# A decoder layer's attention stage: one store for the sums of four heads, and three kinds of stores issued from GpSimd instead of SyncE

## The chip, the cores and the metric

The kernel runs on one core of a Trainium2 chip. The core has a matrix engine (TensorE, in the profile PE; its weight loads are PEld), VectorE (DVE), ScalarE (ACT), GpSimd (POOL) and SyncE (SP), each with an instruction stream of its own, executed in order. They meet only through semaphores. Data moves between DRAM and the on-chip memory, and from one set of partitions to another, by DMA. A DMA is issued as an instruction of one engine's stream and carried out by 16 DMA engines. The metric is device time in microseconds; three runs of the kernel before gave 1806.03, 1810.8 and 1818.87 us, so the median is 1810.8 us.

## The reference

A decoder layer on x of 1024 tokens by 1024 channels, in float32. What matters here is branch A, differential attention with 8 heads of two softmax maps each:

```python
s = jnp.einsum('bqhcd,bkhcd->bhcqk', qblk, kf) * scale
s = s + bias[None, :, None]                    # ALiBi, and -max where the key is later than the query
p = jax.nn.softmax(s, axis=-1)
a = p[:, :, 0] - lam * p[:, :, 1]
out = jnp.einsum('bhqk,bkhe->bqhe', a, vf)
...
a = rms_norm(a, subln_g[l]) * (1.0 - lam_init)      # per head, over its 128 channels
y_attn = a.reshape(B, S, DIFF_V_WIDTH) @ w_attn_branch[l]
...
gates = jax.nn.sigmoid(gate_logits)
mix = gates[:, :, 0] * y_attn + gates[:, :, 1] * y_pool + gates[:, :, 2] * y_mem
x = x + rms_norm(mix @ w_out[l], norm_mix_post[l])
```

Around it stand a pooling branch, a cross attention into 256 memory tokens, and a channel mixer with a convolution. They are untouched.

## The kernel before

Every float32 product is made as three products of a high and a low part (`split` and `mm3`, lines 83 to 96), so a projection of a 128-channel block is 3 x 8 matmuls per 512 tokens (`proj_half`). Results that are too large to stay on chip go through DRAM tensors: `ao_d` (attention outputs, one row block per head), `gate_d` (logits of the first gate), `ss_d` (sums of squares of the attention outputs), `sum_d` (sums of the first map's exponentials) and `r_d` (the scales worked out of the last two).

The attention stage (lines 706 to 958) goes over 8 heads and, in a head, over 4 blocks `b` of 256 queries, each of two halves `u` of 128 queries. `t = 2b + u` numbers the 128-query tiles. For each half:

- `scores` (line 788) multiplies queries with keys for the two maps `c`, adds the bias and takes the negative maximum on VectorE (line 812), and takes the exponential in place on ScalarE (line 817), whose accumulator gives the row sums: `sm[:, 0:1]` for the first map, `sm[:, 1:2]` for the second. Line 819 stores the first column, 128 numbers, to `sum_d` from SP.
- `combine` (line 824) forms z0 - lam * (sum0 / sum1) * z1 on VectorE; the division by sum0 is left for later.

For each block, `turn_weights` (line 836) transposes the weights on TensorE, `weigh_values` (line 852) multiplies them with the values, copies the result `po` to `ao` and stores it to `ao_d` (line 867, 128 KB, 32 times), and squares it. `head_norm` (line 878) sums the squares over the channels with a matmul of ones and stores one row to `ss_d` (line 885, 1 KB, 32 times). After four heads, `load_norms` (line 890) reads both small tensors back and `head_norms` (line 897) works out the scales.

Beside this work the loop weaves fillers for the next head: `queries_keys(h + 1)` (line 737) loads the weights `raw` (line 322, 512 KB for the queries and again for the keys), projects on TensorE, splits on ScalarE and VectorE into `qtmp` and `ktmp`, and moves these by DMA to the partitions where the scores want them (`q<-qtmp`, line 752, 8 transfers a head; `ks<-ktmp`, line 767, 8 transfers a head). `values(h + 1)` loads the head's values (line 732). `gate(dt)` (line 773) projects a 128-channel block of the first gate's logits and stores it in two halves to `gate_d` (line 781, 256 KB, 16 times in all): five blocks during the heads, three after them. The tiles `qtmp`, `ktmp` and `g0` come from one tag with two buffers (`gq`, tag `"t"`), so a tile is free for its next writer when the transfer out of it has landed.

Order: `weave` lists the stages and fillers, and a planner then settles the order of the instructions on each engine before the run; at run time each engine and each queue executes its list in order, and an instruction whose inputs are not ready holds up all that stand behind it. All DMAs of the kernel are issued from SP, so the stores of the attention stage and the loads for the next head stand in one list. An on-chip tile is given to its next user when the semaphore of its last reader, a DMA's landing included, has been seen.

Of the kernel before, what the change touches and what calls it, by code (L numbers as in the profile page):

```python
# [8 lines left out]
F32 = mybir.dt.float32  # L9
F32R = mybir.dt.float32r  # L10
I32 = mybir.dt.int32
AF = mybir.ActivationFunctionType
ALU = mybir.AluOpType
AX = mybir.AxisListType

P = 128
D = 1024
S = 1024
KT = D // P
H4 = KT // 2  # L20
H = 512
NM = 256
NH = 8
# [15 lines left out]
def kernel(  # L39
# [7 lines left out]
    nc = tc.nc  # L47
# [12 lines left out]
    out = out[0]  # L60
# [6 lines left out]
    small = ctx.enter_context(tc.tile_pool(name="small", bufs=6, side="left"))  # L67
# [6 lines left out]
    def bank(shape=(P, H), name="b1"):  # L74
        return ps1.tile(list(shape), F32, tag="b1", name=name)
# [186 lines left out]
    ident = const.tile([P, P], F32, name="ident")  # L262
# [18 lines left out]
    nlam = const.tile([P, 1], F32, name="nlam")  # L281
# [17 lines left out]
    gate_d = dram.tile([KT, P, S], F32, name="gate_d")  # L299
    ao_d = dram.tile([NH, P, S], F32, name="ao_d")  # L300
# [6 lines left out]
    ss_d = dram.tile([NH, S], F32, name="ss_d")  # L307
# [465 lines left out]
    def gate(dt):  # L773

        wh, wl = wsplit(chunk(w_in, C_G + dt * P), [P, KT, P])
        for i in range(2):
            pg = pbank(name="pg0")
            proj_half(pg, wh, wl, i)
            g = gq.tile([P, H], F32, tag="t", name="g0")
            nc.scalar.activation(out=g, in_=pg, func=AF.Copy)  # L780
            nc.sync.dma_start(out=gate_d[dt][:, i * H:(i + 1) * H], in_=g)
            yield

    zts, ats, pns, exps, last, ends = {}, {}, {}, {}, {}, {}

    biases = {}

    def scores(h, b, u):

        qs, ks = qktiles[h]  # L790
        t = 2 * b + u
        n = (t + 1) * P
        parts = 1 if n <= H else 2
        m = n // parts
        q = qs[t // 4]
        ts = slice((t % 4) * P, (t % 4 + 1) * P)
        mx = small.tile([P, 2], F32, tag="mx", name="mx")
        sm = small.tile([P, 2], F32, tag="sm", name="sm")
        z2 = []

        def halves(a):
            return a.rearrange("p (a m) -> p a m", a=parts)

        for c in range(2):
            pss = bank2(name="pss2")
            for i in range(parts):
                keys = ks[c][:, i * m:(i + 1) * m]
                for j in range(2):
                    nc.tensor.matmul(pss[:, i * H:i * H + m], q[:, j, c, ts], keys, start=(j == 0), stop=(j == 1))  # L809
            z = ap_.tile([P, S], F32, tag="z%d" % c, name="z", bufs=3 - c)  # L810
            o = 896 - t * P
            nc.vector.tensor_tensor_reduce(  # L812
                out=halves(z[:, 0:n]), in0=pss.rearrange("p (a m) -> p a m", a=2)[:, 0:parts, 0:m],
                in1=halves(biases[h][:, o:o + n]), scale=1.0, scalar=3.0e38,
                op0=ALU.add, op1=ALU.min, accum_out=mx[:, c:c + 1])
            z2.append(z)
            nc.scalar.activation(out=z[:, 0:n], in_=z[:, 0:n], func=AF.Exp, scale=-1.0,  # L817
                                 bias=mx[:, c:c + 1], accum_out=sm[:, c:c + 1])
        nc.sync.dma_start(out=sum_d[h, t * P:(t + 1) * P].rearrange("(p o) -> p o", o=1), in_=sm[:, 0:1])
        exps[h, b, u] = z2, mx, sm  # L820
        if b == 3 and u == 1:
            qktiles.pop(h)

    def combine(h, b, u):

        z2, mx, sm = exps.pop((h, b, u))
        n = (2 * b + u + 1) * P
        nc.vector.reciprocal(out=mx[:, 1:2], in_=sm[:, 1:2])
        nc.vector.scalar_tensor_tensor(
            out=mx[:, 0:1], in0=mx[:, 1:2], scalar=sm[:, 0:1], in1=nlam, op0=ALU.mult, op1=ALU.mult)  # L830
        last["combine"] = nc.vector.scalar_tensor_tensor(
            out=z2[0][:, 0:n], in0=z2[1][:, 0:n], scalar=mx[:, 0:1], in1=z2[0][:, 0:n],
            op0=ALU.mult, op1=ALU.add)
        zts[h, b, u] = z2[0]

    def turn_weights(h, b):

        zs = [zts.pop((h, b, u)) for u in range(2)]
        ats[h, b] = []
        for k2 in range(b + 1):  # L840
            at = [ap_.tile([P, 4 * P], F32R, tag="aT", name="aT%d" % j, bufs=9) for j in range(2)]
            pt = bank((P, 4 * P), "pta")

            todo = [(kk, u) for kk in range(2) for u in range(2) if (k2, kk, u) != (b, 1, 0)]
            for j, (kk, u) in enumerate(todo):
                k = 2 * k2 + kk
                nc.tensor.transpose(pt[:, j * P:(j + 1) * P], zs[u][:, k * P:(k + 1) * P], ident)
            n = len(todo) * P
            split(at[0][:, 0:n], at[1][:, 0:n], pt[:, 0:n])
            ats[h, b].append(at)  # L850

    def weigh_values(h, b):
        at = ats.pop((h, b))
        vh, vl = vtiles[h]
        bs = slice(b * 2 * P, (b + 1) * 2 * P)
        po = bank((P, 2 * P), "poa")

        parts = [(k, slice(0, 2 * P), at[k // 2], slice((k % 2) * 2 * P, (k % 2 + 1) * 2 * P))
                 for k in range(2 * b + 1)]
        terms = [(part, i, j) for part in parts for i, j in ((0, 0), (0, 1), (1, 0))]  # L860
        last = (2 * b + 1, slice(P, 2 * P), at[b], slice(2 * P, 3 * P))
        terms[1:1] = [(last, i, j) for i, j in ((0, 0), (0, 1), (1, 0))]
        for n, ((k, qs, w, ws), i, j) in enumerate(terms):
            nc.tensor.matmul(po[:, qs], (vh, vl)[i][:, k, :], w[j][:, ws], start=(n == 0), stop=(n == len(terms) - 1))  # L864
        ao = ap_.tile([P, 2 * P], F32, tag="ao", name="ao", bufs=2)
        nc.scalar.activation(out=ao, in_=po, func=AF.Copy)
        nc.sync.dma_start(out=ao_d[h][:, bs], in_=ao)

        sq = ap_.tile([P, 2 * P], F32, tag="sq", name="sq", bufs=1)
        nc.scalar.activation(out=sq, in_=po, func=AF.Square)  # L870
        sqs = [ap_.tile([P, 2 * P], F32R, tag="sq%d" % j, name="sq%d" % j, bufs=1) for j in range(2)]
        nc.scalar.activation(out=sqs[0], in_=sq, func=AF.Copy)
        ends["square"] = nc.vector.tensor_tensor(out=sqs[1], in0=sq, in1=sqs[0].bitcast(F32), op=ALU.subtract)
        pns[h, b] = sqs
        if b == 3:
            vtiles.pop(h)

    def head_norm(h, b):
        sqs = pns.pop((h, b))
        pn = bank((P, 2 * P), "pn")  # L880
        for j in range(2):
            nc.tensor.matmul(pn, ones, sqs[j], start=(j == 0), stop=(j == 1))
        srow = ap_.tile([1, 2 * P], F32, tag="srow", name="srow", bufs=2)
        nc.scalar.activation(out=srow, in_=pn[0:1, :], func=AF.Copy)  # L884
        nc.sync.dma_start(out=ss_d[h:h + 1, b * 2 * P:(b + 1) * 2 * P], in_=srow)

    HG = NH // 2
    hns = {}

    def load_norms(g):  # L890

# [27 lines left out]
    for h in range(NH):  # L919
        if h + 1 < NH:  # L920
            head_bias(h + 1)
        stages = []
        for b in range(4):
            n = 4 * h + b
            stages.append(lambda h=h, b=b: scores(h, b, 0))
            if n >= 1:
                def weights(n=n):
                    combine(*blocks[n - 1], 1)
                    turn_weights(*blocks[n - 1])
                stages.append(weights)  # L930
            stages.append(lambda h=h, b=b: scores(h, b, 1))
            stages.append(lambda h=h, b=b: combine(h, b, 0))
            if n >= 2:
                stages.append(lambda n=n: head_norm(*blocks[n - 2]))
            if n >= 1:
                stages.append(lambda n=n: weigh_values(*blocks[n - 1]))
            if h == HG and b == 1:
                stages.append(lambda: load_norms(0))
            if h == HG and b == 3:
                def norms():  # L940
                    with tc.issue_after(last["combine"].ins):
                        head_norms(0)
                stages.append(norms)
        fillers = []
        if h + 1 < NH:
            fillers += steps(queries_keys(h + 1), 4)
            for n, step in enumerate(steps(values(h + 1), 2)):
                fillers.insert(2 * n + 1, step)
        for dt in GATES[h]:
            fillers += steps(gate(dt), 2)  # L950
        weave(stages, fillers)
    combine(*blocks[-1], 1)
    turn_weights(*blocks[-1])
    head_norm(*blocks[-2])
    weigh_values(*blocks[-1])
    head_norm(*blocks[-1])
# [424 lines left out]
```

## Time and profile before

One execution was profiled. Its own time, 1826.35 us, differs a little from the three timed runs.

| | us |
|---|---|
| median of three runs | 1810.8 |
| profiled execution | 1826.35 |
| its span, first to last instruction | 1824.6 |
| TensorE busy | 1745.2 |
| VectorE busy | 1238.9 |
| ScalarE busy | 863.3 |
| GpSimd busy | 4.4 |
| attention stage, 510 to 973 us of the span | 463 |
| TensorE busy in it | 412.77 |

All times in a profile count from the first instruction. Issuing a DMA and waiting for a semaphore are not counted as busy. The chain of waits starts from the last instruction and goes back, at each step to what released it; a piece called DMA runs from the issue of a transfer to its landing. "SPq" is the instruction queue of SP. A list of waits names the engine and line that waited, what ended the wait, the microseconds in total, how often, and the longest.

### The profile page before, as it was taken

To read this page: it belongs to the slowest core of one execution; us is meant where nothing else is said; L and a number is where in the kernel's file an instruction comes from. 1 tells how busy PE (TensorE), PEld (TensorE's weight loads), DVE (VectorE), ACT (ScalarE), POOL (GpSimd) and SP (SyncE) were. 2 spreads that over 40 slices of the span, in tenths; PEclk is the share of its full clock that TensorE was granted. 3 is DMA by queue.
4 is the path that set the end of the run, shared out by engine and by line. 5 is a ranking of instruction groups with operands and counts; after the bars stand their busy time and mean duration, and the time that the engine had idled before them with its cause. 6 is when DMAs were issued, how large, how long until landed. Compare 5 with 4: busy or idle time off the path is not lost.

```text
span 1824.6 us, 22737 instructions
## 1 busy us (share of the span) xinstructions
PE 1745.2 (96%) x8208; PEld 1451.3 (80%) x8208; DVE 1238.9 (68%) x2159; ACT 863.3 (47%) x1502; POOL 4.4 (0%) x27
## 2 busy tenths in 40 slices
PE   6999999999988899889899999999999999999997
PEld 5888888888866778768787788888888888888886
DVE  8775866666544656646665556676888888878476
ACT  6344454444434545535563333364555555543452
POOL 0000000000000000000000000000000000000000
PEclk9999999999998999989999999999999999999999
DMA  7783454353594666866737566175333433483343
GB/s 244 262 317 131 153 171 152 116 174 115 144 163 111 119 106 114 126 99 118 116 65 233 185 204 173 47 229 175 116 97 117 122 104 96 140 313 116 105 146 130
DMA packets 239430, 271.89 MB, mean 149 GB/s; under 512 B 23681, under 2 KB 173398, under 8 KB 237910
## 3 DMA queue, kind: packets, MB, share of 16 engines
q1 hardware_dynamic: 239318, 270.44, 53.4%
q8 instruction: 65, 1.06, 0.3%
q14 instruction: 47, 0.39, 0.1%
HBM read 176.45 MB, written 68.78 MB: 134 GB/s over the span
## 4 chain that ended last, share of the span: by engine, by line
PE 74%; DMA 14%; DVE 6%; ACT 3%; issue 2%; SPq 1%; DVEq 0%; ACTq 0%
PE pa L94 6%; PE pa L96 6%; PE pa L95 6%; PE pb L94 4%; PE pb L96 4%; PE pb L95 4%; DMA ks<-ktmp 3%; DMA sum_d<-sm 2%; DMA raw<-in_w_in_dram 2%; PE poa L864 2%; PE pss L809 2%; PE pqk L95 2%; PE pqk L94 2%; PE pqk L96 2%; PE pe L96 2%
## 5 line engine op out<-in xcount | busy, mean ns | idle before, releaser
L812 DVE CUSTOM_DVE_ANT_0 z<-pss,hbias 128x256 f32<-128x256 f32 (+7 forms) x128 | 94.2, 753 | 58.3 <-PE pss L809 57.3
L86 ACT ACTIVATE wh<-raw 128x1024 fp32r<-128x1024 f32 (+1 forms) x64 | 60.9, 951 | 132.0 <-PE pqk L95 34.6
L1159 DVE SCALAR_TENSOR_TENSOR cvt<-gv,cols,cvt 128x1023 f32<-128x1023 f32 x88 | 112.5, 1279 | 15.6 <-ACT cvt L1155 14.3
L86 ACT ACTIVATE wpage<-s 128x512 fp32r<-128x512 f32 x120 | 75.2, 627 | 89.9 <-PE pb L96 33.6
L94 PE MATMUL pqk<-hTh,wh 128*128 128x512 f32 x256 | 104.1, 407 | 11.7 <-ACT wh L86 11.7
L809 PE MATMUL pss<-ks,q 128*128 128x512 f32 (+5 forms) x384 | 91.7, 363 | 24.1 <-DMA ks<-ktmp 18.0
L817 ACT ACTIVATE z<-z,mx 128x256 f32<-128x256 f32 (+7 forms) x128 | 98.8, 773 | 32.5 <-DVE mx L812 31.5
L87 DVE TENSOR_TENSOR wl<-raw,wh 128x1024 fp32r<-128x1024 f32 (+1 forms) x64 | 69.6, 1087 | 63.2 <-ACT wh L86 50.2
L87 DVE TENSOR_TENSOR wpage<-s,wpage 128x512 fp32r<-128x512 f32 x120 | 82.1, 690 | 41.2 <-ACT wpage L86 41.1
L94 PE MATMUL pa<-T,wpage 128*128 128x512 f32 x264 | 102.8, 389 | 0.9 <-DVE gv L244 0.9
L95 PE MATMUL pqk<-hTl,wh 128*128 128x512 f32 x256 | 103.2, 403 | 0.0
L96 PE MATMUL pqk<-hTh,wl 128*128 128x512 f32 x256 | 103.1, 403 | 0.0
L96 PE MATMUL pa<-T,wpage 128*128 128x512 f32 x264 | 102.7, 389 | 0.0
L95 PE MATMUL pa<-T,wpage 128*128 128x512 f32 x264 | 102.7, 389 | 0.0
L809 PEld LDWEIGHTS pss<-ks,q 128*128 128x128 f32 x384 | 68.1, 202 | 37.0 <-DVE mx L812 11.5
L86 ACT ACTIVATE page<-blk 128x1024 fp32r<-128x1024 f32 (+1 forms) x42 | 41.4, 988 | 85.5 <-PE pe L95 50.6
L87 DVE TENSOR_TENSOR page<-blk,page 128x1024 fp32r<-128x1024 f32 (+1 forms) x42 | 47.6, 1134 | 39.2 <-ACT page L86 39.2
L94 PE MATMUL pd<-page 128*128 128x512 f32 x176 | 69.3, 394 | 2.0 <-ACT row L1269 2.0
L95 PE MATMUL pd<-page 128*128 128x512 f32 x176 | 69.1, 393 | 0.0
L96 PE MATMUL pd<-page 128*128 128x512 f32 x176 | 68.9, 392 | 0.0
L94 PEld LDWEIGHTS pqk<-hTh,wh 128*128 128x128 f32 x256 | 49.7, 194 | 20.0 <-ACT wh L86 12.0
L864 PE MATMUL poa<-aT,v 128*128 128x256 f32 (+1 forms) x480 | 62.2, 281 | 0.5 <-ACT srow L884 0.5
(383 smaller groups left out, 4877.2 us busy)
## 6 DMA issues: line engine op xcount, KB each, us to landing
raw<-in_w_in_dram SPq DMA_DIRECT2D x32, 512.0 KB
q<-qtmp SPq DMA_DIRECT2D x64, 256.0 KB
wd<-in_w_down_dram SPq DMA_DIRECT2D x22, 512.0 KB
tw_d<-wd SPq DMA_DIRECT2D x11, 1024.0 KB
rawv<-in_w_up_dram SPq DMA_DIRECT2D x22, 512.0 KB
rawu<-in_w_up_dram SPq DMA_DIRECT2D x22, 512.0 KB
ff_d<-cvt SPq DMA_DIRECT2D x22, 512.0 KB
blk<-ff_d SPq DMA_DIRECT2D x20, 512.0 KB
```

The costliest lines, as they stand in the source:

```text
L86: nc.scalar.activation(out=hi, in_=src, func=AF.Copy)
L87: nc.vector.tensor_tensor(out=lo, in0=src, in1=hi.bitcast(F32), op=ALU.subtract)
L94: nc.tensor.matmul(o, ah, bh, start=first, stop=False, skip_group_check=onto)
L95: nc.tensor.matmul(o, ah, bl, start=False, stop=False, skip_group_check=onto)
L96: nc.tensor.matmul(o, al, bh, start=False, stop=last, skip_group_check=onto)
L809: nc.tensor.matmul(pss[:, i * H:i * H + m], q[:, j, c, ts], keys, start=(j == 0), stop=(j == 1))
L812: nc.vector.tensor_tensor_reduce(out=halves(z[:, 0:n]), in0=pss.rearrange("p (a m) -> p a m", a=2)[:, 0:parts, 0:m], in1=halves(biases[h][ ...
L817: nc.scalar.activation(out=z[:, 0:n], in_=z[:, 0:n], func=AF.Exp, scale=-1.0, bias=mx[:, c:c + 1], accum_out=sm[:, c:c + 1])
L864: nc.tensor.matmul(po[:, qs], (vh, vl)[i][:, k, :], w[j][:, ws], start=(n == 0), stop=(n == len(terms) - 1))
L1159: nc.vector.scalar_tensor_tensor(out=cv[:, sh:], in0=u[:, 0:S - sh], scalar=w, in1=cv[:, sh:], op0=ALU.mult, op1=ALU.add)
```

## The change

A tile `sums` of 128 partitions by 8 heads by 8 query tiles is allocated once for the whole stage. The exponential of the first map accumulates into its column `[:, h, t]` instead of into `sm`, which keeps only the second map's sum; `combine` reads the column there. The store of 128 numbers per half (64 in all) goes away. In its place `turn_sums(g)` transposes the 32 columns of four heads on TensorE, copies the result to a row tile on ScalarE and stores it to `sum_d` in one DMA from SP, for the first four heads at the start of the fifth, and for the other four after the last block's `turn_weights`. The stores to `gate_d`, `ao_d` and `ss_d` are issued from GpSimd's queue instead of SP's. The values computed are the same.

```diff
-            nc.sync.dma_start(out=gate_d[dt][:, i * H:(i + 1) * H], in_=g)
+            nc.gpsimd.dma_start(out=gate_d[dt][:, i * H:(i + 1) * H], in_=g)
...
+    sums = ap_.tile([P, NH, KT], F32, name="sums", bufs=1)
...
-        sm = small.tile([P, 2], F32, tag="sm", name="sm")
+        sm = small.tile([P, 1], F32, tag="sm", name="sm")
...
-                                 bias=mx[:, c:c + 1], accum_out=sm[:, c:c + 1])
-        nc.sync.dma_start(out=sum_d[h, t * P:(t + 1) * P].rearrange("(p o) -> p o", o=1), in_=sm[:, 0:1])
+                                 bias=mx[:, c:c + 1], accum_out=sm if c else sums[:, h, t:t + 1])
...
-        nc.vector.reciprocal(out=mx[:, 1:2], in_=sm[:, 1:2])
+        t = 2 * b + u
+        n = (t + 1) * P
+        nc.vector.reciprocal(out=mx[:, 1:2], in_=sm)
         nc.vector.scalar_tensor_tensor(
-            out=mx[:, 0:1], in0=mx[:, 1:2], scalar=sm[:, 0:1], in1=nlam, op0=ALU.mult, op1=ALU.mult)
+            out=mx[:, 0:1], in0=mx[:, 1:2], scalar=sums[:, h, t:t + 1], in1=nlam, op0=ALU.mult, op1=ALU.mult)
...
-        nc.sync.dma_start(out=ao_d[h][:, bs], in_=ao)
+        nc.gpsimd.dma_start(out=ao_d[h][:, bs], in_=ao)
...
-        nc.sync.dma_start(out=ss_d[h:h + 1, b * 2 * P:(b + 1) * 2 * P], in_=srow)
+        nc.gpsimd.dma_start(out=ss_d[h:h + 1, b * 2 * P:(b + 1) * 2 * P], in_=srow)
...
+    def turn_sums(g):
+
+        pt = bank((P, P), "ptn")
+        nc.tensor.transpose(pt[0:HG * KT, :], sums[:, g * HG:(g + 1) * HG].rearrange("p h t -> p (h t)"), ident)
+        row = ap_.tile([HG * KT, P], F32, tag="trow", name="trow", bufs=1)
+        nc.scalar.activation(out=row, in_=pt[0:HG * KT, :], func=AF.Copy)
+        nc.sync.dma_start(out=sum_d[g * HG:(g + 1) * HG].rearrange("h (t p) -> (h t) p", p=P), in_=row)
...
+            if h == HG and b == 0:
+                stages.append(lambda: turn_sums(0))
             if h == HG and b == 1:
                 stages.append(lambda: load_norms(0))
...
     turn_weights(*blocks[-1])
+    turn_sums(1)
     head_norm(*blocks[-2])
```

More of the change, by code (lines that the diff above doesn't have):

```diff
@@ L826, in combine @@
         z2, mx, sm = exps.pop((h, b, u))
-        n = (2 * b + u + 1) * P
-        nc.vector.reciprocal(out=mx[:, 1:2], in_=sm[:, 1:2])
+        t = 2 * b + u
+        n = (t + 1) * P
+        nc.vector.reciprocal(out=mx[:, 1:2], in_=sm)
         nc.vector.scalar_tensor_tensor(
-            out=mx[:, 0:1], in0=mx[:, 1:2], scalar=sm[:, 0:1], in1=nlam, op0=ALU.mult, op1=ALU.mult)
+            out=mx[:, 0:1], in0=mx[:, 1:2], scalar=sums[:, h, t:t + 1], in1=nlam, op0=ALU.mult, op1=ALU.mult)
         last["combine"] = nc.vector.scalar_tensor_tensor(
```

## The prediction

> **What bounds the kernel now.** I read the page first, then stretches of the span, then who waited for whom on TensorE, then the DMA queue of SP. The page says that TensorE is nearly always busy, and that GpSimd (POOL) has next to nothing to do:
>
> ```profile
> span 1824.6 us, 22737 instructions
> PE 1745.2 (96%) x8208; PEld 1451.3 (80%) x8208; DVE 1238.9 (68%) x2159; ACT 863.3 (47%) x1502; POOL 4.4 (0%) x27
> ```
>
> A gain must therefore come from TensorE's idle time or its clock. Nearly all that the diff touches lies in the attention stage, 510 to 973 us, so I asked for that stretch and for three short ones in it (span, busy time of PE, PEld, DVE, ACT, POOL, granted clock, DMA share, GB/s):
>
> ```profile
> 510.00:973.00 463.00, 412.77 (x2199) 352.57 (x2198) 265.51 (x634) 235.68 (x532) 0.00 (x0) 0.94 0.64 111
> 630.00:636.00 6.00, 0.92 (x5) 0.61 (x4) 1.32 (x2) 0.93 (x3) 0.00 (x0) 0.88 0.57 153
> 634.60:641.40 6.80, 5.88 (x20) 5.09 (x21) 3.41 (x13) 3.16 (x9) 0.00 (x0) 0.50 0.81 92
> 788.60:797.10 8.50, 0.11 (x2) 0.04 (x1) 1.38 (x3) 1.57 (x3) 0.00 (x0) 0.68 0.45 97
> ```
>
> TensorE idles 463.00 - 412.77 = 50.2 us there. After an idle piece (630 to 636) it works at half clock (0.50 from 634.6 on), so a stall is paid twice. Over the stage the clock is 0.94: another 0.06 x 463 = 27.8 us. What ended TensorE's idle time in this stage (us, times, longest):
>
> ```profile
> PE pss L809 <- DMA ks<-ktmp: 18.0, 4, 5.1
> PE pta L847 <- DVE aT L87: 12.2, 2, 8.4
> PE pqk L94 <- ACT wh L86: 11.7, 1, 11.7
> PE pss L809 <- DVE mx L812: 6.1, 8, 4.0
> ```
>
> The largest entry is the scores waiting for keys of the next head, which come by DMA from ktmp. Why are they late? SP's queue in order of time (start, duration of the issue, line, transfer, count):
>
> ```profile
> 606.23 0.66 SPq L819 DMA_DIRECT2D sum_d<-sm  x1
> 610.41 0.24 SPq L885 DMA_DIRECT2D ss_d<-srow  x1
> 610.75 0.32 SPq L867 DMA_DIRECT2D ao_d<-ao  x1
> 614.11 0.32 SPq L732 DMA_DIRECT2D v<-v_d  x1
> 614.52 1.63 SPq L819 DMA_DIRECT2D sum_d<-sm  x2
> 616.24 0.24 SPq L885 DMA_DIRECT2D ss_d<-srow  x1
> 616.57 0.32 SPq L867 DMA_DIRECT2D ao_d<-ao  x1
> 618.16 0.38 SPq L322 DMA_DIRECT2D raw<-in_w_in_dram  x1
> 618.64 1.08 SPq L819 DMA_DIRECT2D sum_d<-sm  x1
> 619.94 1.12 SPq L767 DMA_DIRECT2D ks<-ktmp  x2
> 623.55 3.58 SPq L752 DMA_DIRECT2D q<-qtmp  x4
> 627.71 5.17 SPq L767 DMA_DIRECT2D ks<-ktmp  x2
> ```
>
> and the chain of waits over the same time and two later places (start, us to landing, transfer):
>
> ```profile
> 606.23 11.87 DMA sum_d<-sm
> 618.16 9.49 DMA raw<-in_w_in_dram
> 627.71 7.77 DMA ks<-ktmp
> ...
> 721.03 15.76 DMA sum_d<-sm
> ...
> 873.98 16.75 DMA ao_d<-ao
> ```
>
> Count the issues. From the sum store at 606.23 to raw at 618.16 is eight, and raw leaves when that store has landed (606.23 + 11.87 = 618.10). From raw to ks at 627.71 is eight again, and 618.16 + 9.49 = 627.65. The queue behaves as if it had eight slots handed round in order: a transfer waits until the one eight places ahead has landed. A 512-byte sum store holds a slot for 11.87 or 15.76 us, longer than the weight load of 512 KB (9.49), and the keys pay for it. The queue's own waits in the stage agree:
>
> ```profile
> SPq L819 <- ACT z L817: 40.7, 28, 7.8
> SPq L781 <- ACT g L780: 28.4, 9, 5.5
> SPq L885 <- ACT srow L884: 27.2, 12, 3.7
> SPq L752 <- DMA sum_d<-sm: 21.7, 9, 3.7
> SPq L767 <- DMA sum_d<-sm: 14.2, 5, 4.7
> SPq L322 <- DMA sum_d<-sm: 11.7, 7, 3.3
> SPq L894 <- DMA ss_d<-srow: 8.0, 2, 7.8
> SPq L732 <- DMA sum_d<-sm: 8.4, 3, 4.9
> ```
>
> Loads of q, keys, weights and values stood 21.7 + 14.2 + 11.7 + 8.4 = 56.0 us behind landing sum stores, and the queue stood 40.7 + 28.4 + 27.2 = 96.3 us for ScalarE to produce what three of the stores carry.
>
> **The change part by part.**
>
> *Sum stores.* 64 transfers leave SP, and two of 16 KB each take their place. On SP this removes the 40.7 us of waits for exponentials, the 56.0 us of slots, and the issues:
>
> ```profile
> L819 SPq DMA_DIRECT2D sum_d<-sm x64: 319/390/1427, 519.8 to 953.8; - x64
> L847 PE MATMUL pta<-ident,z x288: 270/272/474, 522.7 to 961.0; 128*128 128x128 f32 x144
> L884 ACT ACTIVATE srow<-pn x32: 357/359/375, 534.6 to 968.1; 1x256 f32<-1x256 f32 x32
> ```
>
> 64 x 0.39 = 25 us of issue. None of it is TensorE's time by itself; it counts only through the load it holds up. Added are two transposes and two ScalarE copies: 2 x 0.27 + 2 x 0.36 = 1.3 us, taken wholly on the path (below, 0, since ScalarE is busy 235.68 of 463 us; the extra use of a two-buffer PSUM tag keeps me from taking that).
>
> *Accumulating into columns of a shared tile.* It has as many instructions as before. A wait would be new only if two engines may not touch different columns of one tile at once. The tile mx shows that they may (ScalarE reads column 0 of it while VectorE writes column 1):
>
> ```profile
> 598.88 0.60 ACT L817 ACTIVATE z<-z,mx 128x384 f32<-128x384 f32 x1
> 599.18 0.08 DVE L812 DVE_READ_ACCUMULATOR2_ANT mx<- 128x1 f32 x1
> ```
>
> So it costs nothing; if the whole tile is guarded instead, see the rivals.
>
> *Stores moved to POOL.* 32 ao, 32 ss and, in this stage, 11 gate stores leave SP with their 28.4 + 27.2 us of waits and their slots. On POOL each waits for the same ScalarE copy; behind it on POOL stand only further stores, and POOL is busy 4.4 us in the whole span. What waits for their landing is their source tile's next writer and, far later, the readers in DRAM. The trace has no transfer issued from POOL. From ScalarE's copy to landing I bound it by the 7.77 us of a keys' transfer, which has the 128 KB of an ao store, and the 16.75 of ao itself; I take 10, nearer to the first, since a store on POOL has no loads ahead of it in its queue. At 10 nothing is late. The other five gate stores come after the stage, under TensorE's last gate products, and are read later still: 0. The Trainium skill, "DMA: Bandwidth & Descriptors", section "Latency and other measured facts", puts the first byte at about 1 us from GpSimd against 0.6 us from SP; by that my 10 would be 10.4, and the sum the same.
>
> *What it does for the loads.* With the eight stores from 606.23 to 618.64 gone, raw no longer waits for 618.10: ahead of it stand q and v loads alone. The third ks then is the seventh issue behind raw, not the eighth, and doesn't wait for it. Raw itself would leave right behind v, at 614.5 if v keeps its time and near 607 if v moves up too: 4 to 11 us earlier, where the longest ks stall is 5.1. I take all four ks stalls as gone: 18.0 us. Each is followed by half clock like that of 634.6 to 641.4; at full clock its 5.88 us of work take 2.94: 4 x 2.94 = 11.8 us.
>
> *What stays.* The 12.2 us has its 8.4 at 788.6. Just before, SP stood 7.8 us (L894, group 0's norms) for an ss store, and load_norms still sits on SP, now behind a POOL store and the row of sums: kept. Group 1's norms have the same wait, at the end of the stage, under those gate products: 0. The 11.7 us is a weight load at the stage's start: kept. Of the 6.1 us behind mx, which follow late ks transfers through ScalarE's queue, I take half: 3.0.
>
> Sum: -18.0 - 11.8 - 3.0 + 1.3 = -31.5 us. The profiled execution took 1826.35 us (its span 1824.6 and 1.75 around it), and would take 1794.9. It is 15.5 us above the median of the runs, 1810.8; I subtract from the median: **1779 us**.
>
> **The rivals.**
>
> *All stalls go.* Earlier loads feed every stall: 50.2 + 27.8 = 78 us, 1733 us. For it: every entry but mx hangs on a transfer somewhere behind. Against: the norms load and the first weight load are not stores.
>
> *The transfers are the bound, no change.* If loads land late because the 16 engines are full, issuing them earlier only makes them wait there. For it: a DMA share of 0.64 over the stage and 0.81 from 634.6. Against: 0.57 and 0.45 in the very stalls (630 and 788.6). Then perhaps a fifth of the ks part is won: 0.2 x 29.8 - 1.3 = 4.7 us, 1806 us. The Trainium skill, same page, section "Issuing engines are not separate DMA queues", says that all queues run on the same 16 engines and that issuing from several saves only the issue time. By that rule the change would end here; the trace's eight-slot waits speak of something that the rule leaves out.
>
> *POOL's stores hold tiles, slower.* The gate tile shares two buffers with qtmp and ktmp, of which the stage allocates 7 x 4 + 11 = 39, one per 463 / 39 = 11.9 us. A gate store that takes longer than that makes ScalarE wait for the next but one, in order, with the exponentials behind it. At 16.75 us: 11 x (16.75 - 11.9) = 53 us, 1779 + 53 = 1832 us. It decides from 11.9 + 31.5 / 11 = 14.8 us on. For it: no row shows POOL's speed. Against: it took 16.75 once, in a crowded queue.
>
> *The shared tile is guarded whole.* Then 64 exponentials wait for VectorE's previous read. Priced by the 0.30 us that the two rows above overlap: 64 x 0.30 = 19 us, 1798 us. Against: those rows.
>
> **How the numbers follow.** Chances: forecast 0.60, all stalls 0.12, transfers 0.19, POOL 0.06, guarded tile 0.03. One per cent, 18.1 us, is about what a measurement can tell. Faster by more than that (under 1792.7) are the forecast's case and the first rival, 0.72; same are the transfers and the guarded tile, 0.22; slower is POOL's, 0.06. The forecast's own range is 1762 to 1789 (half of the kept 24 us going with 5 us of clock, or a third of the ks part failing). The range leaves out POOL's case and a quarter of the transfers' above, half of the first rival below: 1745 to 1807 us.
>
> **What would show it.** Right: SP's list of waits has no sum_d, PE's wait for ks falls from 18.0 to under 5, the stage's clock rises above 0.96, the stage is near 432 us long. Wrong: ks waits stay while raw leaves earlier (the transfers bind); ScalarE waits for gate_d or ao_d (POOL); exponentials wait for L829 (the tile). A long wait of SP at load_norms with 8.4 us of PE idle behind it would show that what I kept is kept.

## The result, and the profile after

Four runs of the changed kernel took 1765.77 to 1769.16 us, median 1767.27. Four of the kernel before, the three named at the start and one of 1818.06 us, have a median of 1814.43. The ratio is 0.9746, with an interval of 0.9704 to 0.9788: 2.5% faster. The forecast was 1779 us (1745 to 1807). The profiled execution took 1765.77 us, where that of before took 1826.35: between the two profiles lie 60.6 us, and more than the 46 us of the ratio, since the execution that was profiled before was a long one.

From the page of the kernel after (the third line: packets, MB, share of the 16 engines' time):

```profile
span 1763.9 us, 22651 instructions
PE 1729.2 (98%) x8210; PEld 1438.1 (82%) x8210; DVE 1238.8 (70%) x2159; ACT 861.4 (49%) x1504; POOL 47.4 (3%) x107
q1 hardware_dynamic: 223222, 262.01, 48.0%
```

To compare the stage, I took the same work in both: from the first exponential to the last row of squares' sums, from there to the first matmul of the attention branch's projection (`pya`), and on to its last. Stretches of the span before the change (span, busy time of PE, PEld, DVE, ACT, POOL, granted clock, DMA share, GB/s):

```profile
518.40:968.10 449.70, 399.48 (x2140) 341.52 (x2139) 262.75 (x624) 232.39 (x528) 0.00 (x0) 0.94 0.64 109
968.10:995.30 27.20, 27.20 (x121) 22.51 (x120) 15.04 (x25) 9.23 (x12) 0.00 (x0) 1.00 0.85 272
995.30:1086.50 91.20, 88.22 (x382) 71.22 (x381) 51.36 (x63) 34.85 (x48) 0.00 (x0) 1.00 0.62 196
```

and after it:

```profile
519.10:904.30 385.20, 381.27 (x2142) 326.88 (x2141) 261.94 (x624) 230.84 (x530) 39.20 (x73) 1.00 0.48 127
904.30:931.50 27.20, 27.20 (x121) 22.53 (x120) 14.89 (x25) 9.11 (x12) 3.21 (x6) 1.00 0.85 263
931.50:1025.40 93.90, 89.86 (x382) 72.30 (x381) 52.76 (x64) 37.13 (x50) 0.54 (x1) 0.98 0.59 193
```

The first row of each holds the whole gain. The stage went from 449.70 to 385.20 us, 64.5 less, with the same instructions (2140 and 2142 matmuls: two are new). TensorE's idle time in it fell from 449.70 - 399.48 = 50.2 to 385.20 - 381.27 = 3.9 us, and its busy time from 399.48 to 381.27, because the clock no longer drops (0.94 before, 1.00 after). So 46.3 us are stalls and 18.2 us the slow work behind them. In the third rows 2.7 us come back, all at the start of `pya`: TensorE idles 4.0 us there instead of 3.0, and its clock is 0.98 instead of 1.00. The rest (0.7 us before the stage, 0.4 behind `pya`) is small: -64.5 + 2.7 + 0.7 + 0.4 = -60.7, the difference of the two spans.

Who TensorE waited for after the change, in the stage (us, times, longest):

```profile
PE pss L811 <- DVE mx L814: 3.1, 10, 0.4
PE poa L866 <- ACT srow L886: 0.5, 1, 0.5
PE pqk L94 <- ACT wh L86: 0.4, 1, 0.4
```

All three large rows of before are gone, not only the keys' 18.0 us: the 12.2 us of `pta` as well, and the 11.7 us of `pqk` behind the first weight load have shrunk to 0.4. SP's own waits show why the loads are no longer late:

```profile
SPq L322 <- DVE wl L87: 92.2, 9, 21.4
SPq L732 <- PE pss L811: 43.7, 5, 9.6
SPq L767 <- ACT ktmp L86: 29.7, 8, 5.3
```

SP now waits for a free buffer (L322, weights), for TensorE (L732, the next head's values; the row names a score matmul), or for the keys to be there (L767). It runs ahead of the compute engines. Of waits for `sum_d` one is left, 1.0 us for the new row of sums at `load_norms`. The transfers (KB each, median us from issue to landing, over the whole run and over those transfers whose landing the profile tells):

```profile
raw<-in_w_in_dram SPq DMA_DIRECT2D x32, 512.0 KB, 4.1
ks<-ktmp SPq DMA_DIRECT2D x64, 128.0 KB, 2.4
ao_d<-ao POOLq DMA_DIRECT2D x32, 128.0 KB, 3.6
gate_d<-g POOLq DMA_DIRECT2D x16, 256.0 KB, 2.9
ss_d<-srow POOLq DMA_DIRECT2D x32, 1.0 KB, 2.2
```

This I had not forecast. The weight load that took 9.49 us in the chain before lands in 4.1, the keys' that took 7.77 in 2.4. (The chain picks late transfers, and no median is known for the kernel before. The kernel with the moves alone, below, has medians of 9.9 and 5.5.) The transfers themselves became fast, while the stage moves more bytes per second than before (127 against 109 GB/s) with a smaller share of the DMA engines' time (0.48 against 0.64).

### The profile page after: what moved, and what is told of

Same layout as the page of the kernel before. It is cut to its first block, busy times and chain, and to the rows that moved or that the text cites. A ratio compares the mean times of both kernels' runs of the same rounds, so it can differ in the third digit from the quotient of the medians.

```text
span 1763.9 us, 22651 instructions
## 1 busy us (share of the span) xinstructions
PE 1729.2 (98%) x8210; PEld 1438.1 (82%) x8210; DVE 1238.8 (70%) x2159; ACT 861.4 (49%) x1504; POOL 47.4 (3%) x107
## 4 chain that ended last, share of the span: by engine, by line
PE 70%; issue 18%; DMA 4%; DVE 4%; POOL 2%; ACT 2%; SPq 0%; POOLq 0%; DVEq 0%; ACTq 0%
PE pa L94 7%; PE pa L96 7%; PE pa L95 7%; PE pb L94 5%; PE pb L96 5%; PE pb L95 5%; PE pe L96 2%; PE pe L94 2%; PE pe L95 2%; PE pd L94 2%; PE pd L95 2%; PE pd L96 2%; PE pya L96 2%; PE pya L95 2%; PE pya L94 2%
## 5 line engine op out<-in xcount | busy, mean ns | idle before, releaser
L811 PE MATMUL pss<-ks,q 128*128 128x512 f32 (+5 forms) x384 | 86.7, 348 | 3.1 <-DVE mx L814 3.1
L811 PEld LDWEIGHTS pss<-ks,q 128*128 128x128 f32 x384 | 63.7, 188 | 14.7 <-DVE mx L814 9.5
L866 PEld LDWEIGHTS poa<-aT,v 128*128 128x128 f32 x480 | 59.7, 190 | 2.5 <-ACT srow L886 0.9
```

## The experiments

Two theories stood against each other. By *slots*, the prediction's, a sum store harms because it holds one of eight places in SP's queue for 10 us, so what counts is how many stores stand in SP's list. By *clogging*, a store of 128 separate numbers of 4 bytes harms every transfer that runs at the same time, on whatever queue it was issued, so what counts is that there are such stores. Kernels that are compared directly ran on one chip, together with the kernel before, unless the text says otherwise. The medians of the kernel before were 1808.76 us (beside the kernels of the next section and those with a constant), 1810.73 (beside the first four of the table) and 1809.48 us (beside the rest). Ratios stand with 95% intervals and needn't equal the quotient of two medians.

### One part alone

The sums part alone is the changed kernel with the three moved stores back on SP:

```diff
-            nc.gpsimd.dma_start(out=gate_d[dt][:, i * H:(i + 1) * H], in_=g)
+            nc.sync.dma_start(out=gate_d[dt][:, i * H:(i + 1) * H], in_=g)
...
-        nc.gpsimd.dma_start(out=ao_d[h][:, bs], in_=ao)
+        nc.sync.dma_start(out=ao_d[h][:, bs], in_=ao)
...
-        nc.gpsimd.dma_start(out=ss_d[h:h + 1, b * 2 * P:(b + 1) * 2 * P], in_=srow)
+        nc.sync.dma_start(out=ss_d[h:h + 1, b * 2 * P:(b + 1) * 2 * P], in_=srow)
```

> The sums kept in one tile and stored for four heads at once; the gate, ao and ss stores stay on SP. Computes everything. Theory of slots (SP has eight in order, and a store of 128 four-byte numbers holds one for some 10 us): the slow store is gone and the others land quickly, so most of the gain is kept, 1770 to 1785 us, and SP waits some 60 us for ScalarE's copies. Theory of clogging (a store of 128 four-byte numbers slows the transfers around it, on whatever queue): all of the gain, 1766 to 1772 us, with the weight loads landing in 4 to 5 us as in the changed kernel. Theory that GpSimd's queue is what counts: little of the gain, 1800 us or more.

Measured: 1761.07 us, ratio 0.9725 (0.9657 to 0.9793). The whole gain is there without moving anything to GpSimd, and a few us more. Slots had 1770 to 1785, since 80 stores stay in SP's list; clogging, with 1766 to 1772, was 5 us too high. SP still waits for ScalarE's copies, 80.7 us for the rows of squares' sums and 37.8 us for the gate's in the stage, more than the 60 expected, and the time is the lowest all the same.

The moves alone are the kernel before with those three lines on GpSimd, and the 64 sum stores still on SP.

> The gate, ao and ss stores on GpSimd's queue; the 64 stores of 128 four-byte sums stay on SP. Computes everything. Theory of slots: 75 of some 300 transfers of the stage leave the eight slots and SP no longer waits for their producers, about half of the gain, 1785 to 1800 us. Theory of clogging: next to nothing, 1805 to 1815 us, with weight loads landing in 9 us or more. Theory of GpSimd's queue: nearly all, 1765 to 1775 us.

Measured: 1803.15 us, ratio 0.9951 (0.9923 to 0.9979). Taking 80 of the 144 stores away from SP is worth half a per cent. Neither theory's range holds the time: it lies 2 us under that of clogging (1805 to 1815) and 3 us over that of slots (1785 to 1800). The transfers stay slow in this kernel, those on GpSimd's queue too (KB, median us to landing):

```profile
raw<-in_w_in_dram SPq DMA_DIRECT2D x32, 512.0 KB, 9.9
sum_d<-sm SPq DMA_DIRECT2D x64, 0.5 KB, 9.2
ss_d<-srow POOLq DMA_DIRECT2D x32, 1.0 KB, 8.0
```

The last row speaks against slots by itself. A row of 1 KB in GpSimd's queue, where no sum store stands, takes 8.0 us to land; after the change, in the same queue, it takes 2.2.

### Many pieces, in one place or apart

If clogging is right, it has to come back when such stores are put back into the changed kernel. The first try added 64 stores of 512 bytes from a constant tile to a scratch tensor, as one row of 512 bytes or as a column of 128 numbers:

```diff
+    junk_d = dram.tile([NH, S], F32, name="junk_d")
...
+        nc.sync.dma_start(out=junk_d[h, t * P:(t + 1) * P].rearrange("(o p) -> o p", o=1), in_=ident[0:1, :])
```

> The changed kernel with 64 stores more on SP, one for each half block, each of one row of 512 bytes of a constant tile to a scratch tensor, so that none waits for a producer. Theory of slots: 64 more transfers pass the eight slots, but each lands in some 2 us: 1766 to 1773 us. Theory of clogging: the same as the changed kernel, 1766 to 1770 us, since a row of 512 bytes is one piece. If the mere number of transfers on SP counts: 1785 us or more.

```diff
+        nc.sync.dma_start(out=junk_d[h, t * P:(t + 1) * P].rearrange("(p o) -> p o", o=1), in_=ident[:, 0:1])
```

> As the run with 64 row stores, with one difference: each store takes a column of 128 numbers of four bytes instead of a row of 512 bytes (the same constant tile, no wait for a producer, the same order of instructions on TensorE, VectorE and ScalarE). Theory of slots: each holds a slot for some 10 us, but with the other stores on GpSimd's queue there are slots enough: 1775 to 1790 us, the loads' landings as they are in the changed kernel. Theory of clogging: the loads land in 9 us or more and the stalls come back: 1795 to 1815 us.

Measured: rows 1768.8 us, ratio 0.9766 (0.9708 to 0.9824); columns 1850.11 us, ratio 1.0216 (1.0154 to 1.0278), slower than before. The expectation of the place was wrong. A constant is ready at the start and nothing held the stores in the attention stage, so the planner put all 64 early in the list: they were issued between 36 and 161 us with rows, and between 36 and 245 us with columns. The pair still tells columns from rows, in a stage with other work. That early stretch with rows, and with columns:

```profile
20.00:270.00 250.00, 247.70 (x1223) 204.48 (x1223) 186.34 (x360) 116.73 (x232) 0.60 (x16) 1.00 0.61 204
```

```profile
20.00:270.00 250.00, 183.31 (x856) 148.63 (x856) 123.47 (x260) 75.11 (x161) 0.60 (x16) 0.84 0.75 157
```

With columns TensorE is busy for 183 of 250 us instead of 248, at a clock of 0.84, and the DMA engines are busier (0.75 against 0.61) while they move less (157 against 204 GB/s).

To hold the stores in the attention stage, the next four store the sums themselves, right behind the exponential that makes them. Nothing reads the scratch tensor. One piece of at most 32 bytes from one partition:

```diff
+        nc.sync.dma_start(out=junk_d[h:h + 1, t * P:t * P + t + 1], in_=sums[0:1, h, 0:t + 1])
```

> The changed kernel with 64 more stores on SP inside the attention stage, each after its exponential and of one piece (partition 0's sums of the head so far, 4 to 32 bytes) to a scratch tensor. Theory of clogging (128 four-byte pieces slow everything): no slower than the changed kernel, 1765 to 1772 us. Theory that 64 more transfers in SP's list that wait for ScalarE are what costs: 1785 to 1805 us.

The column of 128 numbers, into one run of 512 bytes of DRAM, as the kernel before stored it:

```diff
+        nc.sync.dma_start(out=junk_d[h, t * P:(t + 1) * P].rearrange("(p o) -> p o", o=1), in_=sums[:, h, t:t + 1])
```

> As the run with one piece, the same order on TensorE, VectorE and ScalarE, but each store takes the column of 128 sums, 128 pieces of four bytes. Theory of clogging: weight loads land in 9 us or more instead of 4, PE waits for keys and weights again, 1790 to 1810 us. Theory of the list: as the run with one piece.

The same column from GpSimd's queue, with SP's list as in the changed kernel:

```diff
+        nc.gpsimd.dma_start(out=junk_d[h, t * P:(t + 1) * P].rearrange("(p o) -> p o", o=1), in_=sums[:, h, t:t + 1])
```

> The changed kernel with the 64 columns stored from GpSimd's queue, so that SP's list and its eight slots are those of the changed kernel, and the order on TensorE, VectorE and ScalarE too. Theory of clogging of the DMA engines: as the columns on SP or a little better, 1785 to 1805 us, the weight loads land in 8 us or more. Theory of slots or of SP's list: 1765 to 1772 us, the loads land in 4 us.

The same column from SP, each number 512 bytes behind the last in DRAM, and later 64 bytes (`P` is then 16 in the tensor's last size):

```diff
+    junk_d = dram.tile([NH, KT, P, P], F32, name="junk_d")
...
+        nc.sync.dma_start(out=junk_d[h, t, :, 0:1], in_=sums[:, h, t:t + 1])
```

> As the columns on SP, but each of the 128 numbers goes to an address 512 bytes from the next, instead of all into one run of 512 bytes. If the writes into one run of addresses hold one another up: the loads land in 4 to 5 us and the time is that of the changed kernel, 1765 to 1773 us. If 128 writes of four bytes are slow by themselves: as the columns on SP, 1790 to 1810 us.

> As the columns spread by 512 bytes, with the 128 numbers 64 bytes apart, so that eight fall into each run of 512 bytes. If what holds them up is a block of 64 bytes or less: 1765 to 1773 us, landing in 2 to 3 us. If it is a block of 512 bytes or more: eight at one place instead of 128, a landing of 3 us or more and 1770 to 1790 us.

| added to the changed kernel, 64 times | median us | ratio to before | interval |
|---|---|---|---|
| one piece, SP | 1767.98 | 0.9735 | 0.9686 to 0.9785 |
| 128 x 4 bytes, in 512 bytes, SP | 1805.05 | 0.9942 | 0.9915 to 0.9969 |
| 128 x 4 bytes, in 512 bytes, GpSimd | 1807.45 | 0.9980 | 0.9945 to 1.0015 |
| 128 x 4 bytes, 512 bytes apart, SP | 1770.42 | 0.9743 | 0.9693 to 0.9793 |
| 128 x 4 bytes, 64 bytes apart, SP | 1769.81 | 0.9778 | 0.9736 to 0.9819 |

The last row was measured on another chip than the four above it; the changed kernel took 1768.12 us there. The column on GpSimd came out 2 us above the range that clogging had for it. With 64 bytes, where eight numbers still share each 512 bytes, the time lies in the range expected for a block of 64 bytes or less, but only 0.2 us under that for 512. One of the four executions of the kernel with 512 bytes took 7995.52 us, and why it was so long stays unexplained. The table's 1770.42 is the median of all four; that of the other three is 1769.6.

The kernels with a piece and with columns on SP give TensorE, VectorE and ScalarE the same instructions in the same order, and the three with columns on SP have the same DMAs in the same order in SP's list too: only the addresses in DRAM differ. The kernel with columns on GpSimd has the changed kernel's own order on TensorE, VectorE and ScalarE and in SP's list. So neither the planner's order nor a place in the queue can be what sets them apart. The transfers, and the queue's total (packets, MB, share), with the column in one run of 512 bytes:

```profile
q1 hardware_dynamic: 232438, 262.05, 51.2%
```

```profile
raw<-in_w_in_dram SPq DMA_DIRECT2D x32, 512.0 KB, 6.8
junk_d<-sums SPq DMA_DIRECT2D x64, 0.5 KB, 10.0
```

with the numbers 512 bytes apart:

```profile
q1 hardware_dynamic: 232438, 262.05, 48.0%
```

```profile
raw<-in_w_in_dram SPq DMA_DIRECT2D x32, 512.0 KB, 4.2
junk_d<-sums SPq DMA_DIRECT2D x64, 0.5 KB, 2.2
```

with 64 bytes, the landing of the stores alone:

```profile
junk_d<-sums SPq DMA_DIRECT2D x64, 0.5 KB, 2.7
```

and in one run again, from GpSimd's queue:

```profile
raw<-in_w_in_dram SPq DMA_DIRECT2D x32, 512.0 KB, 8.9
junk_d<-sums POOLq DMA_DIRECT2D x64, 0.5 KB, 9.9
```

In one run the column takes 10 us to land, and the weight loads beside it slow down from 4.2 to 6.8 and 8.9 us. These medians cover the whole run; from 525 to 975 us alone the loads into `raw` have medians of 10.4 us with columns on SP, 9.4 on GpSimd, 4.2 spread by 512 bytes, and 4.1 in the changed kernel. Spread, with the same packets and bytes, the column lands in 2.2 to 2.7 us and costs little: 1770.42 us against 1767.98 with one piece. Slots add nothing that shows: on SP, where the column holds them, it costs 37 us against the kernel with one piece, and on GpSimd, where it holds none of SP's, 39. TensorE's waits follow. With the column on GpSimd, where SP's list holds none of these stores, its first row of the stage is the old one:

```profile
PE pss L812 <- DMA ks<-ktmp: 14.6, 4, 4.7
```

against 18.0 us before the change. The stage's length tells the same in one row for each kernel: the 32 rows of squares' sums, the first and the last start. With the moves alone:

```profile
L884 ACT ACTIVATE srow<-pn x32: 354/358/376, 534.1 to 936.8; 1x256 f32<-1x256 f32 x32
```

after the change, 369.0 us from 535.3 to 904.3:

```profile
L886 ACT ACTIVATE srow<-pn x32: 356/358/375, 535.3 to 904.3; 1x256 f32<-1x256 f32 x32
```

and with columns on SP in one run, on GpSimd in one run, and on SP 512 bytes apart:

```profile
L888 ACT ACTIVATE srow<-pn x32: 356/357/376, 535.4 to 942.4; 1x256 f32<-1x256 f32 x32
```

```profile
L888 ACT ACTIVATE srow<-pn x32: 356/357/374, 535.3 to 946.6; 1x256 f32<-1x256 f32 x32
```

```profile
L888 ACT ACTIVATE srow<-pn x32: 356/357/374, 537.1 to 906.1; 1x256 f32<-1x256 f32 x32
```

By the row quoted in the prediction, the kernel before took 968.1 - 534.6 = 433.5 us. Columns in one run put back 407.0 - 369.0 = 38 us on SP and 42 us on GpSimd; spread, 369.0 - 369.0 = 0. The moves alone have 936.8 - 534.1 = 402.7 us, which looks like 31 us won; but the execution of before that was profiled took 1826.35 us and that of the moves 1798.48, while their medians are less than 6 us apart.

Which packets are slow? From the records of single packets between 510 and 973 us I worked out their time on a DMA engine. The 4-byte packets took 10 ns on average in one run and 9 ns spread: they aren't the slow ones. Their neighbours were. Packets of 512 bytes took 52 ns on average in one run (the longest 4314 ns) and 30 ns spread (1412); packets of 4096 bytes 300 ns (7062) and 195 ns (1359). The medians are the same in both, 27 ns and 159 ns, so a few packets became very long and most did not change. So the cost falls on whatever else an engine has to carry while these stores are under way.

### What the moves to GpSimd cost on top

The sums part alone had come out below the changed kernel, but not beside it on one chip. It was run again beside the changed kernel and a kernel with the store of squares' sums alone on SP:

```diff
-        nc.gpsimd.dma_start(out=ss_d[h:h + 1, b * 2 * P:(b + 1) * 2 * P], in_=srow)
+        nc.sync.dma_start(out=ss_d[h:h + 1, b * 2 * P:(b + 1) * 2 * P], in_=srow)
```

> The sums alone, with the gate, ao and ss stores on SP, once more beside the changed kernel on one chip. If the moves to GpSimd cost time: 1759 to 1763 us, 4 us or more below the changed kernel. If the first difference was the chip's: within 2 us of it.

> The changed kernel itself, to stand beside the two others on one chip: 1765 to 1770 us if the moves cost some 6 us against the sums alone.

> The changed kernel with the 32 ss stores back on SP; ao and gate stay on GpSimd's queue. Computes everything. The kernel with the sums alone came out some 6 us below the changed one. If that is the landing of the last ss store, which the second group's norms wait for behind the stage (2.2 us from GpSimd's queue against 1.1 from SP's): 1760 to 1763 us. If the gate stores or the number of transfers on GpSimd make it: 1765 to 1769 us, as the changed kernel.

Measured: sums alone 1763.49 us, ratio 0.9741 (0.9704 to 0.9778); the changed kernel 1768.12, 0.9769 (0.9731 to 0.9806); squares' sums on SP 1766.14, 0.9762 (0.9724 to 0.9800). The intervals against the kernel before overlap, since that kernel spreads. The runs themselves don't: sums alone took 1761.45 to 1763.94, the changed kernel 1765.50 to 1770.68. With the moves the kernel takes 4.6 us more. The kernel in between (1765.31 to 1770.41) overlaps with the changed one, so the store of squares' sums is 2 us of it at most, and not told from nothing.

The stage itself is as long in both (385.5 us for sums alone, from 518.4 to 903.9, and 385.2). The profiles differ behind it, where `pya` starts; the changed kernel beside it, and sums alone:

```profile
930.00:950.00 20.00, 16.40 (x59) 12.34 (x58) 11.99 (x10) 8.30 (x10) 1.08 (x2) 0.83 0.86 300
```

```profile
930.00:950.00 20.00, 16.29 (x69) 12.37 (x68) 11.18 (x9) 8.10 (x9) 0.00 (x0) 1.00 0.85 279
```

In 20 us TensorE does 59 matmuls where it does 69 with sums alone, at a clock of 0.83 instead of 1.00. At full clock ten matmuls take some 16.29 x 10 / 69 = 2.4 us, half of the 4.6. Two executions of one kernel differ there nearly as much: the first profile of sums alone has 77 matmuls in these 20 us, and the first of the changed kernel 60. The cause isn't settled. SP issues the load of the last squares' sums at 907.01 us in the changed kernel, at 905.83 with their store on SP and at 905.46 with sums alone, but the middle kernel has the low clock there too (0.91). And the planner gave the three kernels different orders of TensorE's matmuls in just this stretch, so the 4.6 us may be the order's and not GpSimd's. The other half isn't placed, and the gate stores and the output stores weren't tried apart.

## Why the prediction was right, and where it wasn't

**Direction and range: right.** Faster by over 1% had 0.72, and 1767.27 lies between 1745 and 1807. It also lies inside the forecast's own range (1762 to 1789). That is closer than the reasons deserve, and in part luck: the forecast kept two stalls that went, and the basis below hid a part of it.

**The bound: right.** TensorE's idle time and clock in the attention stage were all there was to win, and the rows of that stretch held it. The gain came as 46.3 us of idle time and 18.2 us of slow work. Of the terms, the 18.0 us for the keys and the 3.0 of mx (6.1 to 3.1) came as forecast, the slow work was 18.2 us instead of 11.8, and of the 12.2 and 11.7 us that were kept only 0.4 is left. The four things named as signs came: no wait for a sum store on SP (the 1.0 us left is for the new row), no wait for ks, a clock of 1.00, and a stage below the 432 us forecast (463 - 64.5 = 398.5 on that window).

**The step that failed: the eight slots.** "A 512-byte sum store holds a slot for 11.87 or 15.76 us, longer than the weight load of 512 KB (9.49), and the keys pay for it." The count of eight fits the rows, and the waits were there. But I took both durations as given, and asked only who stands behind whom. The question to ask was why 512 bytes take longer than 512 KB. The same cause made the store and the load slow. With columns on GpSimd no slot of SP's is held, and the keys are late by 14.6 us all the same; with columns on SP but spread, the slots are held just as often, though for 2.2 us each instead of 10, and nothing is late. The 96.3 us in which SP stood for ScalarE's copies were no cost either: with the sums alone SP stands longer for the gate and the squares' sums, and the time is the best of all.

**"What stays": wrong, by the same step.** The 12.2 us were kept because `load_norms` would still make SP wait for a landing store, and the 11.7 us because they hang on a weight load. Each hung on a transfer that was slow to land, as the chain of waits before the change shows (start, us to landing, transfer):

```profile
533.93 15.87 DMA raw<-in_w_in_dram
782.54 12.44 DMA ks<-ktmp
```

The first is the load behind the 11.7 us (a sum store that SP issued at 533.55 also stood right ahead of it in the list), the second the keys' transfer behind the 8.4 us. SP issued it 4 us after it had left `load_norms`, and it took 12.44 us to land; how much of the 8.4 us SP's wait added isn't shown. After the change such transfers land in 4.1 and 2.4 us by the median. With columns on SP put back, the wait for the first weight load is back too, at 12.9 us (4.4 with columns on GpSimd). (At group 0's `load_norms` SP still stands 3.4 us for a landing store, where it stood 7.8, but nothing on TensorE waits behind it.) So in its outcome it was the first rival that came true, "all stalls go", given 0.12, though by faster transfers more than by earlier loads. Its price of 78 us was too high: 3.9 us of idle time stay, and 27.8 us for the clock charged the clock loss over the idle time as well, where 18.2 us of slow work were measured. On the scale of the two profiles 60.7 us were saved, which is 29 more than the forecast's 31.5 and 17 less than that rival's 78.

**The basis.** I subtracted what I read in an execution of 1826.35 us from a median of 1810.8. The runs of the kernel before reach from 1797.77 to 1827.95 us, those of the changed kernel from 1765.50 to 1770.68, so the stalls are likely what makes the former spread, and the profile of a long execution shows more stall than the median run has. Between the medians 47 us were saved (1814.43 - 1767.27), about three quarters of the profile's 60.7. This made a term that was half too small in the profile look a third too small in the time.

**Turning the sums: right.** Forecast 1.3 us; two transposes and two copies take 2 x 0.277 + 2 x 0.261 = 1.1 us:

```profile
L895 PE MATMUL ptn<-ident,sums x2: 270/277/284, 719.8 to 898.2; 128*32 128x128 f32 x2
L897 ACT ACTIVATE trow<-ptn x2: 256/261/266, 720.5 to 898.5; 32x128 f32<-32x128 f32 x2
```

**The shared tile: right.** In the stage the exponentials wait on VectorE only for the negative maximum (29.0 us in 43 waits), never for the instruction of `combine` that reads `sums`, and the sums alone made the whole gain.

**The stores on GpSimd: the sign was wrong.** They were costed at 0 and counted as a part of what frees the loads. From ScalarE's copy to landing was bounded by 7.77 and 16.75 us and taken as 10; from issue to landing it is 2.2 to 3.6 us by the median, so the rival in which they hold tiles (from 14.8 us on) didn't come up. But alone they bring 0.5%, and on top of the sums the kernel with them takes 4.6 us more, by the queue or by the planner's order. The Trainium skill, "DMA: Bandwidth & Descriptors", section "Issuing engines are not separate DMA queues", says that issuing from several engines saves only the issue time. I had set the eight slots against it; the moves alone (ratio 0.9951), and the column that does the same harm from GpSimd's queue, agree with the rule.

**The rival "transfers are the bound": half right.** It had the DMA share of 0.64 for it, and I spoke against it with the share of 0.57 and 0.45 inside two stalls. The engines were indeed what made the loads late. What it missed is that the removed stores were what filled them: the same loads need a share of 0.48 now. Its answer to the forecast, that issuing earlier only makes the loads wait there, was not tried, since the transfers themselves changed.

## What to carry to other kernels

Look at small transfers by their landing time, not their bytes. If a store of half a kilobyte takes longer to land than a load of half a megabyte beside it, ask what its pieces do to the others before you ask who stands behind it in the queue, and try it as one row (here by a transpose on TensorE), or with its pieces spread in DRAM (nothing read the spread numbers back here, so what that costs isn't measured). Another queue doesn't help, and the best version measured here leaves the other three stores on SP: 1761 to 1763 us, with the sums part alone.

## What the runs showed of the hardware

A store of 128 numbers of 4 bytes into one run of 512 bytes of DRAM takes about 10 us to land in these runs (medians of 9.2 to 10.8), whether from SP or GpSimd. 64 of them add about 37 us to this kernel in the attention stage (1767.98 to 1805.05) and 81 us near its start (1768.8 to 1850.11). With the same numbers 64 or 512 bytes apart the store lands in 2.7 or 2.2 us, and the kernel is within 3 us of the one with one piece (1767.98) or with none (1768.12). So neither the number of packets nor their size does it by itself, but that they fall close together in DRAM; spacings between 4 and 64 bytes weren't tried.

Why that is so, no run shows. The Trainium skill, "DMA: Bandwidth & Descriptors", section "Specifications", says that transfers below 512 bytes are done as read-modify-write. By itself that would burden the spread stores as much, and they cost nothing; that many such writes to the same bytes' neighbourhood wait for each other, and hold the engines that carry them, would fit the long packets of their neighbours, but is only argued.
